# Two tiles' depthwise taps by 64 channels and two token phases, ahead of two chunk-B pairs, with the modulation products of the second column group close together

## The chip, the core and the metric

One core of a Trainium2 chip runs the whole kernel, as one program with one launch. The metric is the device time of that program in microseconds, as the median of three runs. Engines are named as in the profile: TensorE (PE, with PEld for its weight loads), VectorE (DVE), ScalarE (ACT), GpSimd (POOL), SyncE (SP, which only issues DMAs).

## What is computed

Two residual layers on a sequence of 1024 tokens with 1024 channels. Layer 0 mixes tokens with a convolution module, layer 1 with pooling; each is followed by a SwiGLU network. All of the change is in layer 0's convolution module and in the modulation vectors of layer 0:

```python
mod = c_act @ ada_w[i] + ada_b[i]
sh_m, sc_m, g_m, sh_f, sc_f, g_f = jnp.split(mod, N_ADA, axis=-1)
...
def conformer_conv(h, w1, b1, w_dw, b_dw, ln_g, ln_b, w2, b2):
    u = h @ w1 + b1
    a, g = jnp.split(u, 2, axis=-1)
    u = a * jax.nn.sigmoid(g)
    u = lax.conv_general_dilated(            # causal, 31 taps, each channel alone
        u, w_dw[:, None, :].astype(u.dtype),
        window_strides=(1,), padding=[(CONV_WIDTH - 1, 0)],
        dimension_numbers=("NWC", "WIO", "NWC"),
        feature_group_count=D_MODEL) + b_dw
    u = jax.nn.silu(layer_norm(u, ln_g, ln_b))
    return u @ w2 + b2
```

## The kernel before

**Tiles.** Channels lie on the 128 partitions, so 1024 channels are 8 tiles; tokens are cut into chunk A (0 to 511) and chunk B (512 to 1023). A matmul is one product of a 128x128 weight block with 512 tokens. For precision every product is done three times (`products`, L485): weight and activation are each split into a high and a low half, and high x high, high x low and low x high are summed in PSUM.

**Weights.** `load_weight` (L468) brings 512 KB by a SyncE DMA (L471), takes the high half with a ScalarE CAST and the negated copy with a ScalarE ACTIVATE, and adds the original to that copy with an accumulating DMA that GpSimd issues (L477). Five converted weights (`W_BUFS`, tile w) and three raw ones (`RAW_BUFS`, tile raw) fit at a time.

**The convolution module.** `conv_in` (L713) computes a tile of u for a chunk: a "half" of 8 x 3 products into a bank a, a second half into a bank g (the two are a pair, each half has its own weight), then `conv_glu` (L694) forms a * sigmoid(g). The 31 taps follow. For most tiles they are a `Taps` task (L776): VectorE, and GpSimd with ScalarE's products (tiles ca, pa, pr), do one tap after the other. For two tiles of chunk A TensorE does taps with diagonal weights (`pe_taps`, L749), 8 taps to a weight of 512 KB: for tile 6 every second of them (15), the others staying with VectorE, and for tile 7 all 31. When all tiles of chunk A have their taps, `layer_norm_silu` (L849) sums them, takes the mean with one matmul (mean), the variance (var), the reciprocal root (rstd), and makes v, which the output projection `conv_out` (L912, banks y) reads.

**Modulation.** `ada_columns` (L426) multiplies c with the columns of the modulation weights on TensorE: per vector 8 products of 256 columns (bank ada), each with a 512 KB weight that SyncE loads (tile adaw, two buffers, `ADA_BUFS`). `columns_done` (L449) turns the row into columns with two small matmuls (adac). Vectors 2 and 3 are made while the convolution runs, 4 and 5 later.

**What sets the order.** TensorE's order is the order in which the program is written. A list of units (`unit`, `run_units`) holds the big products; after every few of them `pace` (L220) lets tasks take steps. A task says how long it wants to wait in a planner's clock (`LOAD`, `DELAY`): in `ada_columns` "load" is 4.0 us between two modulation products. The other engines' order is made from this by a scheduler when the program is built; each engine then runs its own list in order, as does SyncE's DMA queue. The units around the change are written at L1580 to L1587:

```python
    conv_in(*[(A, p) for p in some], None, *[(B, p) for p in some])
    put("ln_a", lambda: layer_norm_silu(A), True)
    rest = list(range(KT - 1 - SHARE))
    for p in rest[: len(rest) - HOLD - HOLD_LN]:
        conv_in((B, p))
    for p in PE_TAPS:
        for u in pe_taps(p):
            unit(*u)
```

`some` is tiles 6 and 7, done for chunk A and then for chunk B with the same four weights; the next two tiles of chunk B are 0 and 1.

## Time and profile before

| | us |
|---|---|
| median of three runs | 1740.39 (1738.10 to 1740.81) |
| profiled execution | 1738.56 |
| its span, first to last instruction | 1736.8 |
| TensorE busy in it | 1701.5 |
| VectorE, ScalarE, GpSimd busy in it | 1301.8, 788.3, 464.2 |

The granted TensorE clock is 0.996 of full speed over the span. In a row of the timeline the first two columns are the start and the length of a stretch of equal instructions, x counts them, and the bracket says how long the engine stood idle before it and who released it. A matmul of this kind is written as two instructions, its weight load (PEld) and the product. The length of a stretch reaches to the modelled end of its last instruction, some 0.07 us into the next; work is therefore counted from start to start. L122 is the helper that records every instruction of VectorE, ScalarE and GpSimd, L144 the one for matmuls, so rows are told apart by their tiles.

### The profile page before, as it was taken

How to read it: one execution, taken by the hardware profiler on the slowest of the kernel's cores; microseconds unless marked ns; L12 is line 12 of the kernel's file. 1: busy time of each engine (PE TensorE's matmuls, PEld its weight loads, DVE VectorE, ACT ScalarE, POOL GpSimd, SP SyncE). 2: the span in 40 equal slices, each digit the busy share in tenths (PEclk: the TensorE clock that was granted, in tenths of full speed). 3: DMA queues.
4: the chain of work that ended last, by engine and by line, in shares of the span. 5: the costliest groups of instructions: out<-in, count | busy, mean ns of one | idle time of the engine just before them, and what ended most of it. 6: DMA issues, size and time to landing. Idle time of an engine off the chain costs nothing.

```text
span 1736.8 us, 21673 instructions
## 1 busy us (share of the span) xinstructions
PE 1701.5 (98%) x7746; PEld 1386.7 (80%) x7746; DVE 1301.8 (75%) x1878; ACT 788.3 (45%) x1080; POOL 464.2 (27%) x547
## 2 busy tenths in 40 slices
PE   7999999999998999999999999999999999999997
PEld 5777777778886888888888888888788888888887
DVE  8899898899658787887665987848677666555655
ACT  3668686876545233333223347457333333222213
POOL 2588777794001121221110301111111111000001
PEclk9999999999999999999999999999999999999999
DMA  7958987736776888887886837887777574656461
GB/s 291 300 159 236 231 232 193 209 110 198 250 227 182 269 277 244 285 247 254 312 274 214 268 113 223 241 291 202 247 219 219 167 220 141 259 206 207 166 239 56
DMA packets 111453, 385.44 MB, mean 222 GB/s; under 512 B 12145, under 2 KB 14321, under 8 KB 111346
## 3 DMA queue, kind: packets, MB, share of 16 engines
q1 hardware_dynamic: 74832, 256.11, 41.4%
q0 software_dynamic: 35424, 126.89, 29.5%
q8 instruction: 61, 1.00, 0.2%
q10 hardware_dynamic: 1090, 1.05, 0.2%
q14 instruction: 46, 0.38, 0.1%
HBM read 315.85 MB, written 63.96 MB: 219 GB/s over the span
## 4 chain that ended last, share of the span: by engine, by line
PE 87%; DVE 5%; DMA 3%; issue 3%; POOL 1%; ACT 1%; SPq 0%; DVEq 0%; POOLq 0%; ACTq 0%
PE dn L144 26%; PE a L144 22%; PE e L144 12%; PE p L144 11%; PE y L144 6%; PE g L144 3%; PE first L144 3%; PE tap L144 2%; DMA raw<-in_wgu_dram 2%; POOL pa L122 1%; PE ada L144 1%; DMA adaw<-in_adan_dram 1%; PE rstd L144 1%; DVE t L122 1%; DVE w L122 1%
## 5 line engine op out<-in xcount | busy, mean ns | idle before, releaser
L122 ACT CAST w<-raw 128x1024 fp32r<-128x1024 f32 x269 | 281.8, 1050 | 499.4 <-PE dn L144 222.6
L144 PE MATMUL dn<-g,w 128*128 128x512 f32 (+1 forms) x2184 | 484.7, 383 | 1.7 <-DVE g L122 1.0
L144 PEld LDWEIGHTS dn<-g,w 128*128 128x128 f32 x2184 | 399.7, 188 | 82.2 <-DVE g L122 1.3
L122 DVE TENSOR_TENSOR w<-raw,w 128x1024 fp32r<-128x1024 f32 x197 | 244.3, 1243 | 72.8 <-ACT w L122 71.5
L144 PE MATMUL a<-n,w 128*128 128x512 f32 x1056 | 248.0, 390 | 1.1 <-DVE n L122 0.7
L144 PE MATMUL p<-h,w 128*128 128x512 f32 x1056 | 244.1, 390 | 0.9 <-DVE h L122 0.7
L122 POOL TENSOR_TENSOR pa<-pa,pr 128x512 f32<-128x512 f32 x160 | 228.9, 1510 | 22.8 <-ACT pr L122 19.8
L144 PEld LDWEIGHTS a<-n,w 128*128 128x128 f32 x1056 | 197.7, 188 | 44.8 <-DVE n L122 2.2
L144 PEld LDWEIGHTS p<-h,w 128*128 128x128 f32 x1056 | 197.3, 188 | 43.8 <-DVE h L122 1.5
L122 DVE SCALAR_TENSOR_TENSOR x<-dn,gains,x 128x512 f32<-128x512 f32 (+1 forms) x200 | 138.5, 725 | 95.2 <-PE dn L144 95.1
L122 DVE SCALAR_TENSOR_TENSOR ca<-u,vecs,ca 128x512 f32<-128x512 f32 x245 | 169.9, 746 | 0.5
L144 PE MATMUL a<-t,w 128*128 128x512 f32 x528 | 126.5, 395 | 5.7 <-DVE w L122 2.9
L144 PE MATMUL e<-b,w 128*128 128x512 f32 x528 | 123.7, 390 | 1.6 <-DVE t L122 1.0
L144 PE MATMUL e<-t,w 128*128 128x512 f32 x528 | 123.2, 389 | 0.0
L144 PEld LDWEIGHTS a<-t,w 128*128 128x128 f32 x528 | 100.4, 191 | 28.5 <-DVE w L122 4.2
L122 ACT ACTIVATE pr<-u,vecs 128x512 f32<-128x512 f32 x160 | 108.0, 716 | 26.5 <-POOL pa L122 19.8
L144 PEld LDWEIGHTS e<-b,w 128*128 128x128 f32 x528 | 98.9, 188 | 22.9 <-DVE t L122 1.4
L1090 POOL DMA_DIRECT2D raw<-in_wgu_dram x43 | 38.1, 886 | 292.9 <-DMA raw<-in_wgu_dram 129.0
L144 PEld LDWEIGHTS e<-t,w 128*128 128x128 f32 x528 | 99.1, 188 | 20.6
L161 POOL DMA_DIRECT2D gd<-g x76 | 46.9, 619 | 192.5 <-DVE g L122 188.7
L144 PE MATMUL y<-v,w 128*128 128x512 f32 x384 | 89.2, 391 | 0.5 <-DVE v L122 0.5
L144 PEld LDWEIGHTS y<-v,w 128*128 128x128 f32 x384 | 71.5, 188 | 17.5 <-issue 1.6
(164 smaller groups left out, 1971.4 us busy)
## 6 DMA issues: line engine op xcount, KB each, us to landing
raw<-in_wgu_dram SPq DMA_DIRECT2D x132, 512.0 KB, 4.9
raw<-in_wdn_dram SPq DMA_DIRECT2D x88, 512.0 KB, 7.2
gd<-g POOLq DMA_DIRECT2D x76, 512.0 KB, 7.1
g<-gd SPq DMA_DIRECT2D x76, 512.0 KB, 5.9
adaw<-in_ada_dram POOLq DMA_DIRECT2D x48, 512.0 KB, 7.1
raw<-in_wgu_dram POOLq DMA_DIRECT2D x43, 512.0 KB, 7.1
raw<-in_w_dram SPq DMA_DIRECT2D x36, 512.0 KB, 6.6
adaw<-in_adan_dram SPq DMA_DIRECT2D x32, 512.0 KB, 5.5
```

The lines of the kernel that those rows point to most:

```text
L122: self.last = self.order(getattr(self.eng, name)(out, *args, **kw))
L144: last_mm[0] = nc.tensor.matmul(out, lhsT, rhs, start=start, stop=stop, skip_group_check=more).ins.name
L161: return order(nc.gpsimd.dma_start(*a))
L1090: d = order(nc.gpsimd.dma_start(w[i], wgu[l, fp, src], accum_op=ADD))
```

## The change

**Taps by phases.** Both tiles, 6 and 7, now have all their taps on TensorE, in another form. The function `phases` splits u into a high and a low half, puts even tokens ahead of odd ones, and moves, with four DMAs on SyncE's queue, 64 channels and both phases onto the 128 partitions (tile ph, one for each half g of the channels). A weight of 128x128 then does two taps at once for both phases, so 16 shifts of 256 columns stand for 31 taps of 512. Per tile that is 2 halves x 16 shifts x 3 products and four weights. The result goes back through a ScalarE copy, four DMAs and a ScalarE ACTIVATE that interleaves the phases.

**Places.** Tile 6's four tap units now stand ahead of chunk B's tile 0, tile 7's ahead of its tile 1; before, both stood behind the two.

**Modulation products.** Between the second norm and the end of chunk B's tiles 6 and 7 (`dense`) the planner's gap between two products is 0.8 us instead of 4.0. The turning into columns of vectors 2 and 3 becomes a task of its own that starts 14 us later ("behind"), and the vector's last step is set off from its matmuls ("spread"). The delayed third vector (`held`) is gone. The wait for VectorE's taps of chunk A no longer moves the planner's TensorE clock (`aside`), and the mean is put where VectorE's and ScalarE's clocks say, plus 1.0 ("mean").

```diff
-PE_TAPS = {6: 15, 7: CW}
+PE_TAPS = (6, 7)
 DIAGS = 8
-LOAD = {"load": 4.0, "slow": 6.0, "next": 4.0, "dots": 4.0}
+SHIFTS = (CW + 1) // 2
+LOAD = {"load": 4.0, "dense": 0.8, "behind": 14.0, "slow": 6.0, "next": 4.0, "dots": 4.0}
...
-    def finish(*these):
-        forced[0] = True
+    def finish(*these, aside=False):
+        forced[0], was = True, clock["PE"]
...
         forced[0] = False
+        if aside:
+            clock["PE"] = was
...
+                elif said == "mean":
+                    self.until, self.mark = max(clock["V"], clock["S"]) + 1.0, None
...
-            yield "load"
+            yield "load" if not dense[0] else "dense"
...
-            if k == KT - 1 and (j != 3 or not held[0]):
+            if k == KT - 1 and j < 4:
+                T["ada", j] = Task(columns_done(j, acc), False, 0)
+                T["ada", j].free = True
+            elif k == KT - 1:
                 yield from columns_done(j, acc)
-            elif k == KT - 1:
-                held_back.append((j, acc))
...
-        yield "spread"
+        yield "behind" if j < 4 else "spread"
         cols = bank("adac")
         for h in range(2):
             matmul(cols[:, 4 * h : 4 * h + 4], rows[:, h * P : h * P + P], quarters, start=True, stop=True)
+        yield "spread"
...
-        if ch.i == 0 and PE_TAPS.get(p) == CW:
+        if ch.i == 0 and p == KT - 1:
 
             V_.scalar_tensor_tensor(ba, ba, V("conv_b1", p), sg, op0=ADD, op1=MUL)
...
             S_.copy(uhalo[:, p, :], ba[:, ch.n - HALO :])
+            for q in PE_TAPS[:-1]:
+                phases(q, st["u", 0, q][:, HALO:])
+            phases(p, ba)
             return
...
+    def phases(p, src):
+
+        both = block("h0", "us")
+        parts = [both[:, i].rearrange("p (f s) -> p f s", f=2) for i in range(2)]
+        src = src.rearrange("p (s f) -> p f s", f=2)
+        S_.copy(parts[0], src)
+        V_.tensor_tensor(parts[1], src, parts[0].bitcast(F32), op=SUB)
+        st["us", p] = []
+        for g in range(2):
+            rows = block("h0", "ph")
+            G_.memset(rows[:, :, : HALO // 2].bitcast(F32), 0.0)
+            for f in range(2):
+                sync.dma_start(rows[64 * f : 64 * f + 64, :, HALO // 2 : HALO // 2 + 256].bitcast(F32),
+                               both[64 * g : 64 * g + 64, :, 256 * f : 256 * f + 256].bitcast(F32))
+            st["us", p].append(rows)
...
-                b, wt = st["tap", p], take()
-                for q, j in enumerate(js):
-                    full = PE_TAPS[p] == CW
-                    o = (CW - 1 - j) // 2 * 2 if full else CW - 3 - j
-                    c = j + o if full else 0
-                    products(b[:, o:], wt, q, [v[:, c : c + A.n - o] for v in st["us", p]], j == groups[0][0], j == groups[-1][-1])
+                b, wt, rows = st["tap", p], take(), st["us", p][g]
+                for q in range(DIAGS):
+                    m = first + q
+                    products(b[:, 256 * g : 256 * g + 256], wt, q, [rows[:, a, m : m + 256] for a in range(2)], m == 0, m == SHIFTS - 1)
                     if q % 4 == 3:
                         pace()
...
+                if i == 2 * halves - 1:
+                    back = block("h0", "ph", F32)
+                    S_.copy(back[:, 0], b)
+                    for h in range(2):
+                        for f in range(2):
+                            sync.dma_start(back[64 * h : 64 * h + 64, 1, 256 * f : 256 * f + 256], back[64 * f : 64 * f + 64, 0, 256 * h : 256 * h + 256])
+                    S_.activation(st["u", 0, p][:, HALO:].rearrange("p (s f) -> p f s", f=2), back[:, 1].rearrange("p (f s) -> p f s", f=2),
+                                  AF.Identity, bias=V("conv_bdw", p))
...
-        yield "soon" if ch.i else "stats"
+        yield "soon" if ch.i else "mean"
         b = bank("mean")
...
-    for p in rest[: len(rest) - HOLD - HOLD_LN]:
+    for q, p in zip(PE_TAPS, rest[: len(rest) - HOLD - HOLD_LN]):
+        for u in pe_taps(q):
+            unit(*u)
         conv_in((B, p))
-    for p in PE_TAPS:
-        for u in pe_taps(p):
-            unit(*u)
-    unit(lambda take: held.__setitem__(0, True))
-    unit(lambda take: finish(T["ada", 0]))
-    unit(lambda take: finish(*(T["taps", 0, p] for p in range(KT) if PE_TAPS.get(p, 0) < CW)))
+    unit(lambda take: finish(T["ada", 0], T["ada", 2], T["ada", 3]))
+    unit(lambda take: finish(*(T["taps", 0, p] for p in range(KT) if p not in PE_TAPS), aside=True))
```

The diagonal weights on the host are laid out to match. The order of the instructions moves at three places on which the prediction rests. First TensorE before, from the end of chunk B's tiles 6 and 7 (g_1306) through tile 0 (a_1423) to the taps of tile 6 (tap_1649) and tile 7 (tap_1745); w is a converted weight, adaw a modulation weight:

```order
L144 MATMUL g_1306<-h_774,w_950 128x512 x3
L144 MATMUL ada_1283<-adaw_1341,ccols 32x256 x4
L144 MATMUL a_1423<-h_767,w_960 128x512 x3
...
L144 MATMUL ada_1283<-adaw_1514,ccols 32x256 x4
L144 MATMUL tap_1649<-us_1201,w_1475 128x512 x3
...
L144 MATMUL ada_1283<-adaw_1580,ccols 32x256 x4
...
L144 MATMUL tap_1745<-us_1195,w_1541 128x512 x6
```

And now, from the middle of the gate half of chunk B's tile 7 (g_1332) through tile 6's taps (tap_1464) to tile 0 (a_1637):

```order
L137 MATMUL g_1332<-h_770,w_950 128x512 x3
L137 MATMUL ada_1250<-adaw_1352,ccols 32x256 x4
...
L137 MATMUL ada_1250<-adaw_1377,ccols 32x256 x4
L137 MATMUL tap_1464<-ph_1199,w_960 128x256 x12
L137 MATMUL ada_1250<-adaw_1411,ccols 32x256 x4
...
L137 MATMUL tap_1464<-ph_1199,w_1452 128x256 x24
L137 MATMUL tap_1464<-ph_1203,w_1458 128x256 x24
L137 MATMUL tap_1464<-ph_1203,w_1467 128x256 x24
L137 MATMUL a_1637<-h_767,w_1506 128x512 x3
```

The taps have moved ahead of tile 0, they take four weights of 24 products of 256 columns, and a modulation product (ada) stands at every half of a half instead of at every half, the last one inside tile 6's taps. Second ScalarE before, at chunk B's tile 6 (g_1207 is its gate half; x_79 to x_86 are the residual's blocks, to which gate_b is added):

```order
L122 ACTIVATE x_84<-x_84,gate_b 128x512 x2
L122 COPY uhalo<-a_1079 128x30
L122 ACTIVATE pr_1295<-u_649,vecs 128x512
L122 ACTIVATE t_1301<-g_1207,vecs 128x512
L122 CAST w_1415<-raw_1413 128x1024
L122 ACTIVATE w_1415<-raw_1413 128x1024
```

And now, at the end of chunk B's tile 7 (g_1332), with the two weights of the pair behind tile 6's taps (w_1506, w_1512) and the first of tile 7's taps (w_1546):

```order
L115 ACTIVATE t_1447<-g_1332,vecs 128x512
L115 CAST w_1506<-raw_1504 128x1024
L115 ACTIVATE w_1506<-raw_1504 128x1024
L115 ACTIVATE x_80<-x_80,gate_b 128x512 x2
...
L115 COPY t_1487<-ada_1250 128x256
L115 ACTIVATE x_85<-x_85,gate_b 128x512
L115 CAST w_1512<-raw_1510 128x1024
L115 ACTIVATE w_1512<-raw_1510 128x1024
L115 ACTIVATE x_86<-x_86,gate_b 128x512 x2
L115 CAST w_1546<-raw_1544 128x1024
```

Twelve of the residual's additions now stand between the two weights of that pair. Third TensorE before, from the layer norm's rstd to the first output projection (y_2355), with one pair of chunk B between them:

```order
L144 MATMUL rstd_2176<-ident,col_2117 128x128 x4
L144 MATMUL a_2248<-h_767,w_1920 128x512 x3
...
L144 MATMUL ada_1976<-adaw_2110,ccols 32x256 x4
L144 MATMUL g_2249<-h_767,w_2066 128x512 x3
...
L144 MATMUL ada_1976<-adaw_2174,ccols 32x256 x4
L144 MATMUL y_2355<-v_2183,w_2072 128x512 x3
```

And now:

```order
L137 MATMUL a_2265<-h_770,w_1987 128x512 x3
L137 MATMUL rstd_2279<-ident,col_2201 128x128 x4
L137 MATMUL a_2265<-h_771,w_1987 128x512 x3
...
L137 MATMUL ada_2034<-adaw_2172,ccols 32x256 x4
L137 MATMUL g_2266<-h_767,w_2129 128x512 x3
...
L137 MATMUL ada_2034<-adaw_2236,ccols 32x256 x4
L137 MATMUL y_2414<-v_2286,w_2135 128x512 x3
```

rstd has moved from ahead of that pair into the middle of its first half.

68 lines of the change are left out of this document (24 added, 44 removed).

## The prediction

> **What bounds the kernel now.** I read the page first: busy time, then the chain that ended last.
>
> ```profile
> PE 1701.5 (98%) x7746; PEld 1386.7 (80%) x7746; DVE 1301.8 (75%) x1878; ACT 788.3 (45%) x1080; POOL 464.2 (27%) x547
> ...
> PE 87%; DVE 5%; DMA 3%; issue 3%; POOL 1%; ACT 1%; SPq 0%; DVEq 0%; POOLq 0%; ACTq 0%
> ```
>
> TensorE is busy 1701.5 of 1736.8 us and carries 87% of the chain. A change pays only by what it takes off TensorE's own row of work, less the waits that it adds there. So I read next TensorE's timeline where the change sits, from chunk B's first half to the first output projection.
>
> ```profile
> 119.08 5.74 PE L144 MATMUL a<-h,w 128*128 128x512 f32 x24
> 124.66 0.50 PE L144 MATMUL adac<-quarters,t 128*128 128x4 f32 x4
> 125.02 5.69 PE L144 MATMUL g<-h,w 128*128 128x512 f32 x24
> 130.64 0.64 PE L144 MATMUL ada<-adaw,ccols 128*32 128x256 f32 x8
> 131.21 5.74 PE L144 MATMUL a<-h,w 128*128 128x512 f32 x24
> 136.88 0.64 PE L144 MATMUL ada<-adaw,ccols 128*32 128x256 f32 x8
> ...
> 169.18 0.64 PE L144 MATMUL ada<-adaw,ccols 128*32 128x256 f32 x8 [1.03 <-DMA adaw<-in_adan_dram]
> 169.75 5.75 PE L144 MATMUL tap<-us,w 128*128 128x512 f32 x24
> 175.43 0.64 PE L144 MATMUL ada<-adaw,ccols 128*32 128x256 f32 x8
> 176.00 7.75 PE L144 MATMUL tap<-us,w 128*128 128x496 f32 x33
> 183.58 0.51 PE L144 MATMUL adac<-quarters,t 128*128 128x4 f32 x4
> 183.95 18.61 PE L144 MATMUL tap<-us,w 128*128 128x508 f32 x81
> 202.39 5.61 PE L144 MATMUL a<-h,w 128*128 128x512 f32 x24
> ...
> 208.50 1.12 PE L144 MATMUL mean<-acc,ones 128*128 128x512 f32 x2
> ...
> 228.96 1.16 PE L144 MATMUL rstd<-ident,col 128*128 128x128 f32 x8
> 229.87 5.71 PE L144 MATMUL a<-h,w 128*128 128x512 f32 x24
> ...
> 242.32 5.29 PE L144 MATMUL y<-v,w 128*128 128x512 f32 x22
> 248.09 0.73 PE L144 MATMUL y<-v,w 128*128 128x512 f32 x2 [0.47 <-DVE v L122]
> ```
>
> From 119.08 to 242.32 each piece starts where the last ends. The only waits are 1.03 us for a modulation weight and 0.47 us for the last low half of v. A chunk-B half (24 products) takes 5.67 us (131.21 to 136.88), a modulation product 0.57 (130.64 to 131.21), a pair of adac products 0.36 (124.66 to 125.02).
>
> **The taps.** Tile 6's 15 taps and tile 7's 31 now take three passages, 5.68 + 7.58 + 18.44 = 31.70 us for 138 products (from start to start of the next piece). The change does 2 tiles x 2 halves x 16 shifts x 3 = 192 products of 256 columns. The trace has that shape at the kernel's end, with its weight loads:
>
> ```profile
> L144 PE MATMUL dn<-g,w 128*128 128x256 f32 x144 | 17.9, 284 | 0.0
> ```
>
> ```profile
> L144 PEld LDWEIGHTS dn<-g,w 128*128 128x128 f32 x2184 | 399.7, 188 | 82.2 <-DVE g L122 1.3 <-ACT g L122 0.9 <-DVE x L122 0.7
> ```
>
> 144 of them kept TensorE busy 17.9 us: 124 ns each, with a new weight for every product, as here. So 192 x 0.1243 = 23.9 us, **-7.8**.
>
> **The wait at 169.18** goes, since the modulation products now all stand before tile 6's second tap group: **-1.0**. In exchange they stand close.
>
> **Modulation loads (new wait).** Let E be the end of chunk B's share of tiles 6 and 7. From 119.08 stand its four halves (22.7), six modulation products (3.4) and one adac pair (0.4): E = 145.6. Products now follow each other after half a half: 2.84 + 0.57 = 3.4 us apart, where they were 6.24 apart (130.64 to 136.88). Two buffers hold their weights, so a load may take from the product that frees its buffer to the second next one, some 6.1 us. What a load takes now depends on company; first the stretch until 143 us, then the one after it.
>
> ```profile
> 119.00:143.00 24.00, 24.00 (x120) 18.55 (x116) 23.93 (x37) 21.01 (x34) 18.23 (x19) 1.00 0.40 112
> 143.00:176.00 33.00, 31.97 (x170) 23.11 (x169) 30.75 (x46) 25.77 (x35) 28.28 (x26) 1.00 1.00 276
> ```
>
> ```profile
> DMA to landing us min/median/max: 3.3/3.4/5.6
> ```
>
> ```profile
> w<-in_wdg_dram POOLq DMA_DIRECT2D x5, 512.0 KB, 9.2
> adaw<-in_adan_dram SPq DMA_DIRECT2D x4, 512.0 KB, 9.2
> ...
> w<-in_w_dram POOLq DMA_DIRECT2D x2, 512.0 KB, 8.0
> ```
>
> The last two columns are the DMA share and GB/s: 0.40 and 112 in the first, saturated at 276 in the second; a modulation load of 512 KB lands in 3.4 us there (median) and in 9.2 here. The change fills the first stretch: between 125.4 and 147.6 fall six modulation loads, three raw loads, three accumulating loads (0.524 MB each) and tile 7's four shuffles (0.13 MB each), 6.8 MB. At 276 GB/s that is 24.6 us in a stretch of 22.2: **+2.4**. Bounds: nothing at 3.4 us, since that is under 6.1; at 9.2 us the spacing is (9.2 + 0.3 to issue + 0.6 for the product) / 2 = 5.0 instead of 3.4, 1.6 x 6 = 9.9 us. I take 2.4, nearer the first, because only three accumulating loads (POOLq) fall here, against the seven listed for the saturated stretch. What waits is a product in TensorE's own row, so everything behind it does. On SyncE's queue tile 7's shuffles stand ahead of a modulation load, but their data (about 130) is there before that load's buffer is free (132).
>
> **Weights for pairs and taps.** Tap weights now last 24 x 0.124 = 3.0 us instead of 5.7, and eight are needed instead of six. Each costs ScalarE a CAST and an ACTIVATE, GpSimd an issue, and an accumulating load.
>
> ```profile
> 131.12 7.46 ACT L122 ACTIVATE x<-x,gate_b 128x512 f32<-128x512 f32 x12
> ...
> 145.32 1.05 ACT L122 CAST w<-raw 128x1024 fp32r<-128x1024 f32 x1
> 146.26 1.07 ACT L122 ACTIVATE w<-raw 128x1024 fp32r<-128x1024 f32 x1
> 147.21 1.34 ACT L122 ACTIVATE pr<-u,vecs 128x512 f32<-128x512 f32 x2
> ```
>
> ```profile
> DMA to landing us min/median/max: 7.0/8.4/11.3
> ```
>
> The pair takes 1.9 us (145.32 to 147.21), an x with its bias 0.61 (7.36/12), and the accumulating loads of this region land in 8.4. Five buffers hold weights, and four are in use until E. The tightest is the gate weight of the pair behind tile 6's taps (w_1512). On ScalarE stand from E: the sigmoid 0.6, the pair for w_1506 1.9, twelve x 7.3, the copy of the modulation row 0.3, then w_1512's own pair 1.9: E + 12.0. Issue 0.4, landing 8.4: E + 20.8. TensorE wants it after two modulation products 1.1, tile 6's taps 11.9, half a pair 5.7 and adac 0.4: E + 19.1. That is 1.7 late, less about 1.0 that the last modulation loads already cost behind E; 0.7. For tile 7 the slack of each weight comes to between 0 and 3 us by the same steps, and I add 0.9: **+1.6**. Bounds: 0 if w_1512 lands in 7.0; at 11.3 for this one and one more of tile 7's, 5.
>
> **The layer norm's end.** TensorE now meets rstd in the middle of a chunk-B half: behind it stand half a half, a whole half and two modulation products up to y, 10.6 us instead of 13.4 (228.96 to 242.32). The work between is the same (8 products by rstd, silu, high and low halves).
>
> ```profile
> 230.94 2.23 ACT L122 ACTIVATE t<-u,vecs 128x512 f32<-128x512 f32 x3 [0.43 <-DVE u L122]
> ...
> 244.75 0.60 ACT L122 CAST v<-t 128x512 fp32r<-128x512 f32 x1
> ```
>
> ```profile
> 230.15 4.87 DVE L122 TENSOR_TENSOR u<-u,rstd 128x512 f32<-128x512 f32 x8 [0.16 <-PE rstd L144]
> ...
> 247.35 0.68 DVE L122 TENSOR_TENSOR v<-t,v 128x512 fp32r<-128x512 f32 x1
> ```
>
> In the new order ScalarE converts a weight (1.9) that waits for the half ahead of y (rstd + 10.0), and only behind it four silus (0.7 each), two casts (0.6) and then VectorE's two last low halves: about rstd + 17.0, where now the last is ready 248.0 - 229.0 = 19.0 behind it. TensorE wants the last low half 5.2 us into y, at rstd + 15.8, and the fifth tile's, GpSimd's, about 1 us earlier than it is made. I take a wait of 2.1 in place of 0.47: **+1.6**; bounds 0.5 (all made as early as TensorE asks) and 3.3 (0.47 + the 2.8 lost).
>
> **At no cost.** VectorE loses tile 6's 16 taps: by the order 11 fewer instructions up to the mean, about 7 us. It does not gate: in the trace its sum ends at 207.6, TensorE takes the mean at 208.5.
>
> ```profile
> 206.13 1.50 DVE L122 TENSOR_TENSOR acc<-acc,u 128x512 f32<-128x512 f32 x2
> ```
>
> Of that work now the last pair's sigmoid comes last: the pair ends near 198 (202.4 less 8.8, plus 4.0 of new waits), the sum near 203, and TensorE takes the mean half a half later than now in its third pair, near 207. That also covers the way back of tile 7 (a copy, four DMAs of 64 KB, an ACTIVATE): its products end some 12 us ahead of the pair's end. In ScalarE's queue behind that ACTIVATE stand tap products, a weight and the copy of the mean; if the cover is gone, each us is a us on the mean. Tile 6's shuffles (about 120) have until E. The count of adac products stays the same.
>
> **Sum.** -7.8 - 1.0 + 2.4 + 1.6 + 1.6 = -3.2. The profiled execution took 1738.56 us (1.8 around its span), so 1735.4; the median of the three runs lies 1.8 above that execution, so 1740.4 - 3.2 = **1737.2 us**. Behind y TensorE's order is unchanged but for adac and a shift of modulation products; the idle time from 290 to 400 us there is 2.1 us, which VectorE's lead may shorten, and I leave that out.
>
> ```profile
> 290.00:400.00 110.00, 107.91 (x509) 84.83 (x508) 100.81 (x138) 84.78 (x122) 96.39 (x74) 1.00 0.60 169
> ```
>
> **Rivals.** *All covers hold* (0.20): the modulation loads meet light traffic and land under 6 us, weights come in time. Then -7.8 - 1.0 + 1.6 = -7.2: 1733. For it: DMA share 0.40 now in that stretch; against: the 6.8 MB.
>
> *The taps give nothing back* (0.15): the four weights of a tile arrive at the pace of their bytes, 1.05 MB at 276 GB/s = 3.8 us against 3.0 of work. Eight x 0.8 = 6.4 instead of 1.6: 1742. For it: the share of 1.00; against: three raw loads and one finished weight wait already, and five buffers.
>
> *Modulation loads starve TensorE* (0.15, slower): if they land in 9.2 us as in the saturated stretch, 9.9 instead of 2.4: 1744.7. It decides from about 9 us on: 1.6 lost at each of six products.
>
> *256 columns don't hide the weight load* (0.05, slower): spacing of 188 ns, the weight load's own duration, 192 x 0.188 = 36.1 us, 4.4 more than now instead of 7.8 less: 1749. Against it stand the 124 ns of the last rows, with the same 188 ns loads. The Trainium skill, "TensorE: Matmul & The Clock Gate", section Back-to-back issue gap, says that the spacing of products is set by weight load and product together, and gives 81 ns at 128 columns and 131 at 512; between them that is an estimate of 98 at 256, and by it the taps would cost 18.8 us after and 18.1 before: no gain at all. The trace has 237 ns at 512 (5.67/24) and 124 at 256, and the measurement decides.
>
> **Numbers.** My forecast has 0.45, own range 1734 to 1740. A measurement here tells 0.2% from no change, 3.5 us: 1736.9 and 1743.9. Faster: the first rival and half of the forecast, 0.42. Same: the other half, and most of the second rival, 0.37. Slower: the last two and the second's tail, 0.21. For 8 in 10: the low end takes in most of the first rival, 1732.0; the high end reaches the third rival's price, 1744.5.
>
> **What would show it.** Right: tap products of 256 columns with a spacing near 124 ns and some 24 us in all; waits for adaw of 1 to 4 us between 125 and 148; a wait of 1 to 2 us in the gate half behind tile 6's taps, released by w's accumulating load; a wait of about 2 us in the first y, released by ScalarE's or VectorE's v. The first y would start near 237.5 instead of 242.3. Wrong: tap spacing near 190 ns; adaw waits over 8 us in all; a mean that waits for VectorE; or new idle time behind 300 us.

## The result and the profile after

The changed kernel takes 1757.55 us (median of 4 runs, 1755.89 to 1757.85) against 1739.24 us for the kernel before (4 runs): a ratio of 1.0103, 95% interval 1.0089 to 1.0117. It is 18 us slower, where 3 us faster was forecast and the range ended at 1744.5.

The page of the profiled execution, busy time and the chain of waits:

```profile
PE 1705.2 (97%) x7800; PEld 1389.4 (79%) x7800; DVE 1301.0 (74%) x1868; ACT 792.7 (45%) x1083; POOL 453.8 (26%) x543
PE 78%; DVE 9%; DMA 6%; ACT 4%; issue 2%; POOL 1%; DVEq 0%; ACTq 0%; POOLq 0%; SPq 0%
```

TensorE's share of the chain fell from 87 to 78%. Waits that transfers, VectorE and ScalarE end have grown in its place (DMA from 3 to 6%, VectorE from 5 to 9, ScalarE from 1 to 4). TensorE's timeline shows which (start, length, what, and in brackets the idle time ahead of it with what ended it):

```profile
139.91 0.64 PE L137 MATMUL ada<-adaw,ccols 128*32 128x256 f32 x8 [2.78 <-DMA adaw<-in_adan_dram]
140.47 4.61 PE L137 MATMUL a<-h,w 128*128 128x512 f32 x12
...
152.62 1.71 PE L137 MATMUL tap<-ph,w 128*128 128x256 f32 x12
156.48 0.64 PE L137 MATMUL ada<-adaw,ccols 128*32 128x256 f32 x8 [2.15 <-DMA adaw<-in_adan_dram]
157.05 10.27 PE L137 MATMUL tap<-ph,w 128*128 128x256 f32 x84
...
178.52 11.59 PE L137 MATMUL tap<-ph,w 128*128 128x256 f32 x96
...
191.19 5.28 PE L137 MATMUL a<-h,w 128*128 128x512 f32 x22 [0.62 <-DMA w<-in_w_dram]
...
199.61 6.74 PE L137 MATMUL g<-h,w 128*128 128x512 f32 x22 [2.68 <-DMA w<-in_w_dram]
...
216.84 1.13 PE L137 MATMUL mean<-acc,ones 128*128 128x512 f32 x2 [1.54 <-DVE acc L115]
...
233.63 1.87 PE L137 MATMUL var<-ones,acc 128*128 128x1 f32 x8 [3.14 <-DVE acc L115]
235.36 5.28 PE L137 MATMUL g<-h,w 128*128 128x512 f32 x12
...
244.01 1.05 PE L137 MATMUL rstd<-ident,col 128*128 128x128 f32 x8
...
254.56 1.20 PE L137 MATMUL y<-v,w 128*128 128x512 f32 x4
...
259.74 0.49 PE L137 MATMUL y<-v,w 128*128 128x512 f32 x1 [0.93 <-DVE v L115]
261.12 1.65 PE L137 MATMUL y<-v,w 128*128 128x512 f32 x3 [0.89 <-POOL v L115]
263.33 3.78 PE L137 MATMUL y<-v,w 128*128 128x512 f32 x8 [0.56 <-DVE v L115]
...
383.59 15.29 PE L137 MATMUL dn<-g,w 128*128 128x512 f32 x59 [1.94 <-DVE g L115]
```

The taps themselves do what was forecast. Their three passages take 152.62 to 154.33, 157.05 to 167.16 and 178.52 to 189.95, 23.25 us for 192 products (121 ns each), where 31.70 stood before: -8.45. The first y waits in five pieces, 3.05 us in all (three of them are shown). Everything else in these lines is a loss, and some of it is not idle time: 12 products of a half take 4.61 us behind the first wait and 5.28 behind the one at the variance, where the row at 145.58 has 3.02 for 12. The windows' clock column says why; first the changed kernel, in three stretches (chunk B's tile 6 to the first y; the first output projection; the first dn products), with PE busy, granted clock, DMA share and GB/s:

```profile
119.72:254.56 134.84, 121.44 (x671) 0.95 0.88 227
254.56:308.79 54.23, 51.19 (x232) 0.94 0.75 184
373.10:398.72 25.62, 23.68 (x97) 0.93 0.15 47
```

The same three of the kernel before:

```profile
119.08:242.32 123.24, 122.21 (x616) 1.00 0.83 218
242.32:291.04 48.72, 48.25 (x240) 1.00 0.84 215
353.26:377.01 23.75, 22.32 (x97) 1.00 0.13 45
```

Two microseconds at a time around the first wait:

```profile
141.00:143.00 2.00, 2.00 (x7) 0.58 1.04 324
143.00:145.00 2.00, 2.00 (x6) 0.57 1.04 252
```

TensorE is back at work at 139.91, and runs near half speed from 141 to 145; from 145 to 147 the figure is 1.00 again. So a wait has a second price. The ledger against before: in the first stretch +11.6 us, made of 12.4 more waiting (13.40 less 1.03), 6.7 of clock (0.05 x 134.84, with up to 0.7 from rounding) and -8.45; in the second +5.5 (waits +2.6, clock 3.3, and one modulation product less, -0.6); from 308.79 to 398.72 +4.0, nearly half of it clock behind one wait of 1.94 for VectorE's g. It starts 0.6 late and 2.4 come back behind 445 us of the kernel before: 19.3, the difference of the spans. Put by kind, and up to 399 us: some 17 us more waiting and about 12 us of clock, with 8.45 of taps against them.

Why the mean and the variance wait is read on ScalarE, and behind it VectorE. ScalarE in the changed kernel, and its copy of the mean before:

```profile
189.01 1.05 ACT L115 CAST w<-raw 128x1024 fp32r<-128x1024 f32 x1 [1.70 <-DMA raw<-in_w_dram]
...
197.16 0.57 ACT L115 COPY ph<-tap 128x512 f32<-128x512 f32 x1
...
215.31 0.75 ACT L115 ACTIVATE u<-ph,vecs 128x512 f32<-128x512 f32 x1 [5.67 <-DMA ph<-ph]
215.96 1.92 ACT L115 ACTIVATE pr<-u,vecs 128x512 f32<-128x512 f32 x3
218.16 1.05 ACT L115 CAST w<-raw 128x1024 fp32r<-128x1024 f32 x1 [0.27 <-DMA raw<-in_w_dram]
...
220.07 0.57 ACT L115 COPY ny<-mean 128x512 f32<-128x512 f32 x1
```

```profile
209.95 0.57 ACT L122 COPY ny<-mean 128x512 f32<-128x512 f32 x1
```

VectorE in the changed kernel, and the last of its sums of squares before:

```profile
216.09 0.69 DVE L115 TENSOR_TENSOR acc<-acc,u 128x512 f32<-128x512 f32 x1 [3.93 <-ACT u L115]
220.67 3.08 DVE L115 TENSOR_TENSOR u<-u,mean 128x512 f32<-128x512 f32 x5 [3.88 <-ACT ny L115]
223.66 2.83 DVE L115 TENSOR_TENSOR acc<-acc,t 128x512 f32<-128x512 f32 x1
...
232.01 1.56 DVE L115 SCALAR_TENSOR_TENSOR acc<-t,acc 128x512 f32<-128x512 f32 x1
```

```profile
219.19 0.69 DVE L122 SCALAR_TENSOR_TENSOR acc<-t,acc 128x512 f32<-128x512 f32 x1
```

Tile 7's products end at 189.95. ScalarE copies the bank 7.2 us later, the four loads of 64 KB then take this long (issue to landing, median):

```profile
ph<-ph SPq DMA_DIRECT2D x4, 64.0 KB, 15.7
```

so u is written at 215.31, 25 us behind the products. TensorE's mean waits 1.54 for it. ScalarE, which stood 5.67, has three tap products and a weight pair queued ahead of the copy of the mean, and the pair's raw weight lands only then; so that copy comes 3.2 us behind the mean (before: 1.45). That is 1.8 us of the variance's lateness and not all of it: the sum of squares that the variance reads is done 16.7 us behind the mean (233.57), where it was done 11.4 behind it (219.88), 2.0 ahead of need. The other 3.6 us pass in VectorE's and ScalarE's own work on that sum (from 223.66 to 233.57, where the kernel before takes from 213.55 to 219.88); what makes it longer no run takes apart. The variance waits 3.14.

### The profile page after: what moved, and what is told of

The parts are those of the page before. It is cut to its first block, busy times and chain, and to the rows that moved or that the text cites. A ratio compares the mean times of both kernels' runs of the same rounds, so it can differ in the third digit from the quotient of the medians.

```text
span 1756.1 us, 21816 instructions
## 1 busy us (share of the span) xinstructions
PE 1705.2 (97%) x7800; PEld 1389.4 (79%) x7800; DVE 1301.0 (74%) x1868; ACT 792.7 (45%) x1083; POOL 453.8 (26%) x543
## 4 chain that ended last, share of the span: by engine, by line
PE 78%; DVE 9%; DMA 6%; ACT 4%; issue 2%; POOL 1%; DVEq 0%; ACTq 0%; POOLq 0%; SPq 0%
PE dn L137 26%; PE a L137 19%; PE e L137 11%; PE p L137 10%; PE y L137 6%; DMA raw<-in_wgu_dram 2%; DMA raw<-in_w_dram 2%; PE g L137 2%; ACT w L115 1%; DVE t L115 1%; DVE w L115 1%; PE first L137 1%; DMA adaw<-in_adan_dram 1%; DVE ca L115 1%; POOL pa L115 1%
## 5 line engine op out<-in xcount | busy, mean ns | idle before, releaser
L115 POOL TENSOR_TENSOR pa<-pa,pr 128x512 f32<-128x512 f32 x154 | 218.2, 1478 | 37.5 <-ACT pr L115 34.3
L115 DVE SCALAR_TENSOR_TENSOR ca<-u,vecs,ca 128x512 f32<-128x512 f32 x238 | 164.0, 746 | 0.2
```

What stands on the lines that cost most here:

```text
L115: self.last = self.order(getattr(self.eng, name)(out, *args, **kw))
```

## Experiments

The first runs set four explanations against each other: several sources of waits, each followed by slow clock (the theory); the close modulation loads as the root of all (A); the way back as the root of all (B); slow clock from something other than waits (C). Later runs add others, D to I, named in their expectations. Medians of the kernel before lie between 1739.3 and 1741.1 in these comparisons, so gains and losses are given as differences of the ratios, times 1740 us. Ratios carry their 95% intervals.

**Modulation products back at their old spacing (spread).**

```
-LOAD = {"load": 4.0, "dense": 0.8, ...
+LOAD = {"load": 4.0, "dense": 4.0, ...
```

> The change whole, but the modulation products keep the spacing of before (4.0 in the planner's clock instead of 0.8), so their loads do not crowd into 125 to 150 us. Theory (TensorE's new waits, each over some 1.9 us followed by a few us at half clock, from several sources): the two waits for adaw (2.78 and 2.15 us) and the slow half behind the first (1.7 us) go, 6.6 us, less up to 2 for modulation products that now stand later: 1751 to 1753, ratio to before about 1.007. Rival A (the crowded modulation loads are at the root of all later lateness, since they push back every other transfer): back to 1738 to 1742, ratio 1.000. Rival B (the way back of the taps through DMA is at the root): no more than 3 us better than the change, 1754 to 1757.

1750.72 us, ratio 1.0052 (1.0038 to 1.0065), 8.9 us better than the change. The waits at 139.91 and 156.48 are gone, and so are those at the mean and the variance; A falls, since 9 us are left. The waits in y remain (4.43 in all), and in front of the mean a modulation weight now waits 4.09 (209.95).

**Close modulation products alone, in the kernel before (before_dense).** The lines of the change that set and read `dense`:

```
+            yield "load" if not dense[0] else "dense"
...
                     finish(T["norm_b"])
+                    dense[0] = True
```

> The kernel before with one part of the change alone: the modulation products of the second column group stand close (0.8 instead of 4.0) during chunk B's share of tiles 6 and 7. No phases, no moved taps. Theory: waits for adaw of 4 to 6 us in all and one stretch of half clock (1.7 us), less the 1.03 us wait that goes: 1744 to 1748, ratio 1.003 to 1.004. Rival A (crowded loads at the root of all): over 1750. Without any loss of clock, and with only half of the traffic (no shuffles): 1740 to 1742.

1738.85 us, 0.9991 (0.9982 to 1.0001): no loss at all. TensorE is busy all but 0.35 of these 129 us, at full clock:

```profile
119.00:248.00 129.00, 128.65 (x646) 1.00 0.84 218
```

Theory and A were both wrong here: I had given the close products a price of their own, and they only hurt beside the rest of the change. Which part of it crowds their loads no run shows alone; with less traffic for the tap weights (lows, below) one wait of 2.26 is left of the two.

**No way back (direct).** The ACTIVATE reads the bank itself; the copy and the loads go.

```
-                    back = block("h0", "ph", F32)
-                    S_.copy(back[:, 0], b)
...
+                    S_.activation(st["u", 0, p][:, HALO:], b, AF.Identity, bias=V("conv_bdw", p))
```

> The change whole, but the taps' results skip the way back: the ACTIVATE reads the bank and writes u without the copy and the four DMAs, which leaves out the putting back of the tokens into their order (the numbers are those of other tokens, the work behind is the same). Theory: ScalarE no longer stands 4.3 and 5.7 us for ph, so the weights behind it come in time (0.62 + 2.68 us of waits and 1.4 of slow clock go), the mean's wait goes (1.5 + 0.4), and about half of the 6.3 us at the variance: 1747 to 1750, ratio 1.005; the adaw waits stay. Rival A (crowded modulation loads at the root of all): 1755 to 1758, no change. Rival B (the way back is the root of all behind 185 us): the waits in the first y go too, 17 us in all: 1739 to 1742, ratio 1.001.

1753.42 us, 1.0070 (1.0058 to 1.0082), 5.7 us better. The time lies between the theory's range and A's, in neither. The waits for w shrink from 3.30 to 0.35 and the mean's goes, as the theory had it. The variance still waits, 3.43: without the way back ScalarE stands 5.15 for the raw weight of that same pair, and the copy of the mean behind it. In y the waits stay (3.16, against 3.05). B falls as the sole cause.

**Both edits (spread_direct).**

> Both at once: modulation products at the spacing of before, and the taps' results without their way back (the putting back of the tokens into their order is left out). Theory (both add traffic and waits of their own, and what they leave behind is the other six tap weights and the first y's waits): the waits for w of the first alone (1.64 + 0.48 + 2.04) mostly go, the 4.1 us for adaw at 210 and the slow clock behind it shrink, the first y keeps 3 to 4.5 us of waits and 2 to 3 of clock: 1742 to 1747, ratio 1.001 to 1.004. If the two gains add up in full (6.8 + 4.1 us off the change): 1746. If they are one and the same: 1750.

1746.77 us, 1.0040 (1.0027 to 1.0053). Within the theory's range, and 7 us are left; the waits in its first y alone sum to 4.4.

**The layer norm's place, in the kernel before (late_mean).** One delay of the planner, 2.75 to 7.0, moves mean, variance and rstd half a half later, so that the order up to y is that of the changed kernel.

```
-DELAY = {"stats": 2.75, ...
+DELAY = {"first": 7.0, "stats": 2.75, ...
...
-        yield "soon" if ch.i else "stats"
+        yield "soon" if ch.i else "first"
```

> The kernel before with one number changed (the planner's delay ahead of the first layer norm's mean, 2.75 to 7.0), so that mean, variance and rstd stand each half a chunk-B half later on TensorE, in the same order up to y as in the changed kernel, and y stands 10.6 instead of 13.4 us behind rstd. Nothing else of the change. As predicted for the change: waits in y of 2.1 instead of 0.5 us: 1742 to 1743 (ratio 1.001). Theory now (what the changed kernel's trace shows there): waits of 3 to 4.5 us in y, and 2 to 2.6 us more through half-rate clock behind them: 1745 to 1747, ratio 1.003 to 1.004. If a later mean costs nothing: 1739 to 1742.

1744.46 us, 1.0029 (1.0017 to 1.0040): 5 us slower, three times the 1.6 of the prediction. Its timeline in the first y:

```profile
244.25 2.79 PE L144 MATMUL y<-v,w 128*128 128x512 f32 x11 [0.33 <-POOL v L122]
247.71 0.50 PE L144 MATMUL y<-v,w 128*128 128x512 f32 x1 [0.68 <-DVE v L122]
249.08 0.97 PE L144 MATMUL y<-v,w 128*128 128x512 f32 x3 [0.86 <-POOL v L122]
251.28 3.22 PE L144 MATMUL y<-v,w 128*128 128x512 f32 x8 [1.24 <-DVE v L122]
```

It starts 10.55 us behind rstd (232.88 to 243.43), waits 3.11 in pieces instead of 0.47 once, and the 8 products of the last line take 3.15 us instead of 1.9: the clock again (0.50 from 252 to 254), behind waits of which none is over 1.3 us.

**The same, undone in the changed kernel (stats).**

```
-        yield "soon" if ch.i else "mean"
+        yield "soon" if ch.i else "stats"
```

> The change whole, but the delay of before ahead of the first layer norm's mean, so that mean, variance and rstd stand at the places of before (13.4 us of products between rstd and y, not 10.6); modulation products stay close. Theory (the order of the layer norm on TensorE has a price of its own, some 9 us on top of the spread modulation products: waits in y and the clock behind them, and the variance): 1747 to 1750. Rival (the layer norm is late by its data, so the wait only moves to the mean): 1755 to 1758.

1745.72 us, 1.0039 (1.0025 to 1.0054): 11 us better than the change, more than the theory had. Its mean now waits 4.48 for VectorE's sum, but nothing waits in the first y:

```profile
215.70 2.07 PE L137 MATMUL mean<-acc,ones 128*128 128x512 f32 x2 [4.48 <-DVE acc L115]
```

One wait of 4.48, with one slow stretch (213.1 to 219.9), is cheaper than 1.54 here, 3.14 at the variance and five in y, with two such stretches. The later wait of 1.94 at 383.59 goes with this edit too.

**That and spread products (spread_stats).** Both edits.

> The change with modulation products at the spacing of before, and with the delay of before ahead of the first layer norm's mean, so that mean, variance and rstd stand at the same places as before and 13.4 us of products lie between rstd and y. Theory (the first y's waits come from that order alone: 4.8 us for it was measured in the kernel before): 1750.7 less 4.5 to 6, plus up to 1.5 for a mean that now waits: 1745 to 1747, ratio 1.003. If the chain of the layer norm is late whatever the order (the wait only moves from y to the mean and the variance): 1749 to 1751.

1741.64 us, 1.0014 (1.0005 to 1.0023), better than either theory. Now the way back is what shows: ScalarE stands 6.49 us for it (204.04), VectorE 7.25 behind ScalarE, and the mean 4.09 behind both (210.73).

**And no way back (spread_stats_direct).** All three.

> Modulation products spread, mean's delay as before, and no way back at all (the putting back of the tokens into their order is left out): what the phases would bring if their results came for nothing. Theory (the shortening of the taps by 8.4 us shows once nothing is late): 1732 to 1736, ratio 0.996 to 0.998. If VectorE or the weights hold it even then: 1738 to 1742, and then the taps on TensorE were not what bounded this stretch.

1733.62 us, 0.9967 (0.9956 to 0.9979): faster than before. With little late the shorter taps show, 5.7 of their 8.45 us, though at the price of leaving the tokens out of order. The first y waits 0.49, as before, and the mean and the variance not at all.

**Waits put in by hand (gaps).** Kernel before; in the second layer's feed-forward each `half` of `down` begins with

```
...
+        matmul(b[:, 0:4], ident, quarters, start=True, stop=True)
+        S_.copy(z[:, 0:4], b[:, 0:4])
+        for _ in range(1 + holes[0] % 6):
+            S_.copy(z, cact[:, :512])
+        matmul(b[:, 4:8], ident, z[:, 0:4], start=True, stop=True)
```

> The kernel before with 22 waits put into TensorE's row during the second layer's feed-forward, where nothing else is late: a small product, a chain on ScalarE of one copy and 1 to 6 more copies of 512 columns, and a small product that reads its end (nothing of the result uses them). Gaps of about 0.6 + 0.5 to 0.55 us for each copy, 1.1 to 3.9 us, some 52 us in all. Theory (a wait over about 1.9 us is followed by some us of granted clock at 0.5): granted clock 1.00 behind the gaps of 1.1 and 1.7, 0.5 for 3 to 7 us behind those of 2.7 and more, each costing 1.5 to 3 us more than itself: 52 + 11 to 15 gaps x 2.3 = 77 to 87 us, 1817 to 1827. Rival C (a wait costs itself; the slow clock of the changed kernel comes from something else there): granted clock 1.00 throughout, about 1791.

1853.12 us, 1.0643 (1.0624 to 1.0662), above the 1827 at which the theory ended, since the gaps came out longer than planned (0.9 to 7.3 us, through ScalarE's queue, 70.3 us in place of 52). The span is 111.6 us longer: those 70.3, 15.7 for the small products, and some 25 by which the products behind the gaps ran longer than the same products elsewhere. Three of them:

```profile
1581.80 0.39 PE L144 MATMUL hole<-t,ident 128*128 128x4 f32 x2 [1.55 <-ACT t L122]
...
1594.42 0.39 PE L144 MATMUL hole<-t,ident 128*128 128x4 f32 x2 [2.20 <-ACT t L122]
...
1623.51 0.39 PE L144 MATMUL hole<-t,ident 128*128 128x4 f32 x2 [3.50 <-ACT t L122]
```

and the granted clock (third figure from the right) behind each:

```profile
1581.80:1583.80 2.00, 2.00 (x8) 0.81 0.99 367
1583.80:1585.80 2.00, 2.00 (x6) 0.50 1.02 416
1594.40:1596.40 2.00, 1.98 (x10) 1.00 0.00 0
1623.50:1625.50 2.00, 1.99 (x7) 0.62 0.00 0
1625.50:1627.50 2.00, 2.00 (x7) 0.53 0.00 0
1627.50:1629.50 2.00, 2.00 (x10) 1.00 0.03 8
```

C falls: waits alone bring the half clock, in a stage where nothing else changed. But my threshold of 1.9 us falls too. Of the 22 gaps, the three of 0.90 cost nothing more; one of two of 1.55, none of four of 2.20 and one of two of 2.38 did; and all eleven from 2.91 up did. Such a loss is 1.7 us, and 2.1 to 3.1 behind the four longest.

Most of that scatter goes once one asks where a gap lies. Read in windows of 0.1 us, the slow spells start and end on a fixed grid with a step of 3.41 us. In the changed kernel they start at 141.31, 199.33, 233.47, 260.77 and 383.65: the later ones are 17, 27, 35 and 71 steps behind the first. The spells of this run lie on such a grid too (1094.92, 1583.02 and 1695.66 are 143 and 33 steps apart). Where the grid lies differs from run to run: late_mean's spell at 251.98 is 32.4 steps behind 141.31. The grid cuts each of the four gaps of 2.20 into parts of at most 1.70; of the two of 2.38, the one that cost has 2.21 within one step, the other 1.55. The two of 1.55 each lie within one step, and the DMA share is near 1 behind both; what tells these two apart stays open.

**Whose traffic? (noada).** Of each group's modulation weights only the first two are loaded and used again, 28 loads of 0.52 MB less.

```
-                ws.append(ada_load(src(*todo[i + ADA_BUFS])))
+                ws.append(w)
```

> The change whole, but of the modulation weights of the first layer's gates and second norm only the first two tiles of each group are loaded and used again for every product, which leaves out 28 loads of 0.52 MB between some 70 and 310 us (the modulation values are those of other weights; every product, conversion and issue else is the same). Theory now (the stretch from 119 to 262 us moves 32.2 MB in 142 us where it moved 28.4 in 129, transfers land 9 to 17 us late, and the engines that wait for them in order hold back TensorE): the waits for adaw, for w, at the mean and at the variance all go, 4.9 + 3.3 + 1.5 + 3.1 us, and the half-rate clock behind them, 6.5; the waits in the first y and the clock behind them, 5 us, stay, since they come from the order: 1736 to 1741. Rival D (the order on ScalarE and VectorE, not the transfers): only adaw's waits and the clock behind them go, 6.6 us: 1749 to 1753.

1754.17 us, 1.0080 (1.0066 to 1.0094). No wait for adaw is left, but others take the place: 3.23 at 169.72 and 3.51 at 198.08 for w, 2.78 at the variance. The theory that total traffic is the root falls; the time is just above D's range. One line of ScalarE's shows what holds the first of these weights:

```profile
152.38 6.85 ACT L115 ACTIVATE x<-x,gate_b 128x512 f32<-128x512 f32 x11
```

11 of the 12 bias ACTIVATEs stand ahead of the gate weight's pair, as forecast for w_1512; in the changed kernel the waits for adaw hide it.

**Who waits for the way back (dve_back).** The instruction with the bias on VectorE instead of ScalarE.

```
-                    S_.activation(st["u", 0, p][:, HALO:].rearrange(...), ..., AF.Identity, bias=V("conv_bdw", p))
+                    V_.tensor_scalar(st["u", 0, p][:, HALO:].rearrange(...), ..., V("conv_bdw", p), None, op0=ADD)
```

> The change whole, but the instruction that waits for the way back of the taps (it adds the bias and writes u in token order) stands on VectorE instead of ScalarE; the transfers are the same. Theory E (ScalarE standing 4.3 and 5.7 us in its order for that transfer is what makes the weights behind it late): the waits for w (0.62 + 2.68) and the half clock behind them (1.4) go, the mean's wait (1.5) stays: 1751 to 1754. Theory F (the transfers themselves are late, whoever waits): no better than the change, 1755 to 1759; VectorE then stands instead, and the waits at mean and variance grow.

1756.98 us, 1.0100 (1.0086 to 1.0113): no gain, as F has it, though not by its waits: neither mean nor variance waits, and a modulation weight waits 6.96 at 218.01 instead. E falls by its waits too: with ScalarE free of that instruction the waits for w are still 1.29 and 2.75.

**Which queue (q and spread_stats_q).** The four loads from ScalarE's own queue.

```
-                            sync.dma_start(back[64 * h ...
+                            order(nc.scalar.dma_start(back[64 * h ...
```

> The change whole, but the four small loads of each tile's way back are issued by ScalarE on its own DMA queue instead of SyncE's, where two loads of 0.52 MB stand ahead of them. Theory H (they land after 10 to 16 us because of what stands ahead of them in their queue): they land in 3 to 6 us, ScalarE stands less than 2 us for them, and the kernel comes to what the one without the way back took, 1752 to 1755. Theory I (all queues share engines that are busy to the full, so that the queue doesn't matter): landings stay above 9 us, 1756 to 1759.

> Three edits to the change: modulation products spread as before, the mean's delay as before, the way back on ScalarE's own queue. With the first two alone 1741.6 was measured; its trace has ScalarE standing 6.5 us for the way back of tile 7, VectorE standing 7.3 us behind that, and the mean waiting 4.1 us for VectorE with 2.6 us of half clock behind it. By theory H those go: 1733 to 1737, ratio 0.997 to 0.998, faster than before. By theory I: 1740 to 1743.

1758.74 us, 1.0111 (1.0096 to 1.0127), and 1744.86 us, 1.0035 (1.0023 to 1.0047). The loads of q, all eight:

```profile
ph<-ph ACTq DMA_DIRECT2D x8, 64.0 KB, 9.9
```

9.9 us against 13.1 on SyncE's queue: for these loads the queue is a small part; where the DMA engines are busy (a share of 0.88 over the whole first stretch of the changed kernel, 1.04 around 142 us) 64 KB lands late from either. So far theory I holds, though the second run is 2 us above its range: its mean waits 7.32 for VectorE. For the loads behind them the queue matters: in q the waits for w shrink from 3.30 to 0.31, while the variance now waits 6.54.

**Tap weights without accumulating loads (lows, spread_lows_soon, spread_low7_soon).** Low parts by subtraction on VectorE or GpSimd: `direct(wdg[...])` for `wdg[...]`; in the last for tile 7 only; the last two with spread products and the mean's delay "soon".

> The change whole, but the low parts of the eight tap weights are made by VectorE or GpSimd (raw less its rounded part) instead of an ACTIVATE on ScalarE and an accumulating load: 4.2 MB less to move between 129 and 187 us, 8 us less on ScalarE, 10 us more on VectorE (8 x 1.24). Theory G (the path of a tap weight, conversion and an accumulating load that lands after 8 to 10 us, is too long for weights that last 2.9 us, and its burst delays the loads behind it): the waits for w (3.3) and the slow clock behind them (1.4) go, adaw's 4.9 shrink, the way back lands sooner; against it the mean stands another half of a half later in the order, so the first y waits longer: 1749 to 1754. If tap weights are not the cause: 1757 or more, as VectorE is fuller.

> Three edits to the change at once: modulation products at the spacing of before; the eight tap weights without accumulating loads (low parts by VectorE or GpSimd); mean, variance and rstd at the places of before. Theory (each takes away its own waits): from 1750.7 for the first alone the waits for w go (4.2 us), the first y's go (4.5 to 6 with the clock), the 4.1 us for adaw at 210 us and its 2.4 of slow clock shrink by half: 1736 to 1740, at least level with before. If VectorE, with 10 us more work ahead of the mean, now sets the mean: 1742 to 1748.

> As the one before it, but only tile 7's four tap weights are without accumulating loads; tile 6's, which fall where VectorE is full, keep theirs. Theory: the wait for the gate weight behind tile 6's taps stays (1.6 us), the rest as there, with 5 us less on VectorE: 1736 to 1741. If VectorE sets the mean in the other one and not here, this one is the faster by 2 to 4 us.

1766.86 us, 1.0159 (1.0143 to 1.0174); 1761.32, 1.0123 (1.0109 to 1.0137); 1754.81, 1.0090 (1.0076 to 1.0105). All three miss their theories, and only the first falls where its alternative has it. VectorE has no room: the mean of spread_lows_soon waits 7.69 for it. And spread_low7_soon, which is 1.1 us ahead of before at the same piece near 312 us (311.07 against 312.18), has chunk B's mean behind 36 products of dn (430.36) instead of 12 (423.26), and the second output projection pays with waits of 3.90 and 2.01. That the planner moved it because VectorE's account is 5 us fuller is my reading; no run shows it alone.

**The way back by TensorE (select, select_dense).** The bank is copied to memory, and a chunk-B tile later four small products put the halves into place.

```
+            for f in range(2):
+                for h in range(2):
+                    matmul(b[64 * h : 64 * h + 64, 256 * f : 256 * f + 256], ident[:, 64 * f : 64 * f + 64],
+                           back[:, 0, 256 * h : 256 * h + 256], start=True, stop=True)
```

> Modulation products spread as before, and the taps' results put back into token order by TensorE instead of by DMA: a copy to memory and, one chunk-B tile later, four small products with pieces of the unit matrix (64 x 256 each, in plain float32) into a bank, from which the ACTIVATE writes u. With that the planner itself puts mean, variance and rstd at the places of before. Nothing is left out. Cost: 8 such products of 256 columns in four passes, estimated from 8 passes of 128 columns for rstd (0.81 us, 8 x 128 columns, so 0.2 us for 256) at 2 to 4 us of TensorE in all. Theory (with the way back out of the DMA queues nothing else is late; without any way back 1733.6 was measured): 1735 to 1738, ratio 0.997 to 0.999. Rival (the stretch is bound by VectorE or by the weights, and the small products add a wait of their own for the copy): 1739 to 1744.

> As the one before it, but with the modulation products close together as in the change: the change whole with one thing altered, the way back by TensorE. Theory (close products cost two waits of 2 to 3 us for adaw and one stretch of half clock, 4 us between the kernels so far, part of which the time saved behind them gives back): 1738 to 1742. If the way back and the layer norm's order that hangs on it are nearly all of the loss: 1735 to 1738, level with the one before it. If close products are a cause of their own behind 190 us too: over 1745.

1741.20 us, 1.0009 (1.0000 to 1.0017), and 1746.35, 1.0036 (1.0025 to 1.0046). The products cost 1.0 us a tile, at the low end of the 1 to 2 expected. In select the mean still waits:

```profile
208.20 1.12 PE L137 MATMUL mean<-acc,ones 128*128 128x512 f32 x2 [1.86 <-DVE acc L115]
```

Of the versions with phases that leave nothing out, select has the lowest ratio (the interval of spread_stats overlaps its own), and it is level with before: its mean stands at 208.20, before at 208.50, so the taps' 8 us end in waits for weights (1.69, 0.91) and in front of VectorE, as the rival in its expectation said. select_dense, the change with only the way back altered (and with it the mean's place), is 11.7 us better than the change, as much as stats. It lies where its expectation says that close products are a cause of their own behind 190 us too; the traces say otherwise. It is 8.1 us behind select at tile 7's taps (182.92 against 174.82), mainly through two waits for adaw (2.84 and 2.35) and the clock behind them, and 6.5 at the mean and at the first y: nothing is lost behind 190.

## Why the prediction was wrong

The gain was forecast rightly, the losses were not. Two steps failed above all: the way back was put at no cost, and every wait was priced at its own length, as if the clock stood still. By terms:

**Taps, -7.8:** right; -8.45 measured, 121 ns a product. The rival of 188 ns falls. The wait at 169.18 went, as forecast. The rows of before were the better guide: the estimate from the Trainium skill, "TensorE: Matmul & The Clock Gate", section Back-to-back issue gap, of 98 ns at 256 columns stays below the measurement.

**Modulation loads, +2.4:** the place was right for one of two waits (2.78 at 139.91; the other, 2.15, came at 156.48, behind the stretch I had named), the size was not: 6.6 with the clock, inside the bounds. The seven loads issued from 122 to 150 us landed in 3.4 to 9.5 us, 5.5 in the median. They alone cost nothing in the kernel before (before_dense), which fits a sum over bytes with phases and tap weights in it; no run tests that sum by itself.

**Weights, +1.6:** 3.3 of waits and 1.4 of clock, at another place. The gate weight behind tile 6's taps, the one I worked out, is late where nothing delays TensorE before it (3.23 in noada, 1.64 in spread); in the changed kernel the waits for adaw hide it, and two behind tile 7's taps are late. ScalarE stands 4.3 us for tile 6's way back ahead of the second of these, an instruction I had not put in its queue, but that is not what holds the weight: its CAST waits 1.70 more for the raw weight, until 189.01. That raw weight is issued at 174.34, behind the four loads of the way back in SyncE's queue, and lands after 14.6 us, in dve_back too. Without those loads in that queue the raw loads land after 8.1 to 9.4 us (direct, q), the same CAST comes at 184.26 and 184.82, and waits for w of 0.35 and 0.31 are left. So the way back makes this weight late through SyncE's queue, as far as these runs show (TensorE is up to 3 us later there in both, which hides a part).

**The layer norm's end, +1.6:** the step of the sum that weighs most. The order was read rightly (10.55 us from rstd to y against 10.6 forecast), and my wait of 2.1 was 3.05 measured. What failed is that a wait costs only itself: the whole output projection lost 5.5, of which 3.3 is clock. late_mean prices the order alone at 5 us, and undoing it (stats) gives 11 back, since the wait at the variance (3.14, less 0.33 left) and the one at 383.59 go with it.

**"At no cost", the way back:** wrong. The step said that tile 7's products end 12 us ahead and cover a copy, four loads of 64 KB and an ACTIVATE. They take 25 us (7.2 to the copy, 15.7 to land), and I gave the loads no landing time of their own, in a stretch that my own rows showed saturated. I had written what is lost if the cover goes, a us on the mean for each us, and gave it no term and no chance. Its mark in the trace is the mean's 1.54, a part of the variance's 3.14 and the late weight just named. Leaving the way back out is worth 5.7 us on the change, and 8.2 once order and spacing are mended (1.0014 to 0.9967).

**Behind the first output projection, left out of the sum:** +4.0 up to 399 us, nearly half of it clock, then 2.4 back.

**What no step had:** the clock. Its rows stood at 1.00 in every stretch I quoted, and I took it for constant. It accounts for about 12 us of the loss: half speed behind waits, which gaps shows that waits alone bring about. The trace has 0.50 as its low value, and its slow spells lie on a grid of 3.41 us. With both agrees what the Trainium skill, "TensorE: Matmul & The Clock Gate", section "What's actually happening", tells of a clock that halves after an idle window of about 3.4 us and of a window that runs free of the program. The same page of the Trainium skill, section "HAM oscillation — how this bites in real kernels", puts the danger at gaps over about 3.4 us: here waits of 1.55, 2.38 and 2.78 us were enough, and the measurement decides.

The sources add up only roughly. Order, spacing and way back, undone one at a time, give 11.1, 8.9 and 5.7 us, 25.7 together; all three at once give 23.7, from 1.0103 to 0.9967. In pairs they give less: spacing and way back 11.0 in place of 14.6, order and spacing 15.5 in place of 20.0; the way back, taken away last, gives 8.2 in place of 5.7. By the intervals a difference of two ratios is uncertain by some 3 us, so these shortfalls are hardly clear of noise. That one wait can hide behind another is read from the traces instead: a weight waits 3.23 in noada where the change has its waits for adaw, and a modulation weight 4.09 in spread where the change has the mean's and the variance's. What stays open is the 2.7 us between 8.45 and the 5.7 that spread_stats_direct gained; its remaining waits for weights (1.75, 0.38, 1.55) and adaw (1.10) are more than that, but none was taken away by itself.

## What to carry to other kernels

Price a new wait on TensorE twice: itself, and from about 1.5 us on the 1.7 us or more of half clock that may follow, by where the wait lies on the grid; several short ones in a row count too (late_mean: 0.86 and 1.24, then 0.50). The grid lay differently in each run looked at, so a forecast gives this price a chance of its own. A step that leaves the compute engine for DMA and comes back is to be costed with the landing times of the stretch where it falls, small as it is, and everything behind it with it, in the waiting engine's queue and in the DMA queue that carries it. And when work is taken out of a bound engine, ask how far the chain behind it (here sum, mean, variance, rstd, silu, first y) can move up: from the mean to the first y it was 33.8 us long in the kernel before, and the sum was done 0.9 us ahead of the mean.

## What the runs showed of the hardware

The granted clock has two values in these rows: windows of 0.1 us show 1.00 or 0.50, and something between only where a spell starts or ends. In the changed kernel the spells behind the waits at 139.91 and 383.59 last 3.4 us (1.7 lost), those at the variance and in the first y 6.8, two steps of the grid; one in gaps lasts 10.2, three steps. The four loads of 64 KB landed in 9.4 to 15.7 us in the median where the DMA share was near 1, no faster than loads of 0.52 MB issued beside them (8.4 to 16.9); in lows, which moves 4.2 MB less, they took 6.1. The longest hand-made chain, one short copy and six long ones on ScalarE, made gaps of 6.9 to 7.3 us where 3.9 was expected: between the copies a weight's CAST (1.04 us) stands in ScalarE's queue, and it waits 1.8 to 2.2 us for its raw load.
